# Strassen rounds of a decoder step: two products accumulated onto read-out PSUM banks, and the order of the seven products changed

## The chip, the cores and the metric

The kernel runs on one NeuronCore of one Trainium2 chip, alone. The metric is device time in microseconds (us) of one execution; several executions are timed and the median is given. Beside the times there is one profiled execution, whose trace is what the rows below are taken from.

## What is computed

One decoder layer for 544 tokens (512 of a prompt, 32 of eight sample streams of 4), all in fp32:

```
h = rmsnorm(x);  proj = h @ w_in
att = differential attention(q, k, v);  y = Mamba-2 mixer(conv(xbc), dt, z)
x = x + concat(att, y) @ w_out
hf = rmsnorm(x)
g = hf @ w_gate ; u = hf @ w_up            # 2048 x 5632 each
g = causal conv of width 3 along the tokens (g)
x = x + (silu(g) * u) @ w_down             # 5632 x 2048
y = rmsnorm(x)
```

The change touches only the three large products of the MLP, `w_gate`, `w_up` and `w_down`, which take the last 1,470 us or so of the span of 2441.0 us.

## The kernel before

**Precision.** A product of fp32 accuracy is made of three TensorE passes. Each operand is split in a high part `hi` (a rounded copy, made by ScalarE) and a low part `lo` (the remainder, a subtraction on VectorE); `mm` (line 157) is called for hi x hi, lo x hi and hi x lo. A weight block of 128x1024 goes through `split2` (lines 1067 to 1069): `whi` on ScalarE, then `wlo` on VectorE. Three `whi` and three `wlo` buffers exist, so the weights of three products can be ready or in use at a time.

**Rounds.** Each MLP product is computed in rounds of Strassen's method in Winograd's form. A round (`wino`, line 1113) takes a 2x2 arrangement of weight blocks and a 2x2 arrangement of activation blocks (two halves of 272 tokens each) and forms four output blocks with seven block products instead of eight. The activation blocks `B11, T1, T2, B21, T3, B22, T4` (`T` are sums of blocks) stay in SBUF for many rounds; the weight sums are formed anew for each round by the generator `wino_weights` (line 1071), from four quarters that a DMA brings: `a11`, `s1 = a21+a22`, `s2 = s1-a11`, `a12`, `a11-a21`, `a12-s2`, `a22`, in the order in which the products use them. The first two sums of a round are on VectorE (`wx<-wx`), on GpSimd (POOL) only for the first two rounds of each sequence; the later two (`wx<-wraw,wx`, `wx<-wx,wraw`) are on VectorE.

There are 68 rounds: 44 for gate and up (22 pairs; a product is 8 blocks deep, 24 matmuls of 128x272), then three passes over `w_down` with 8 rounds each (`PASSES`, 7, 7 and 6 blocks deep, 21, 21 and 18 matmuls a product). One product takes one PSUM bank. The bank comes from a ring of three (`half()`, tag `po`) for six of the products; `T1` has a bank of its own, `sB` and `sc` in turn.

**Combining the products.** Let P(X) be the product with block X. The four outputs are (0,0) = P(B11)+P(B21); (1,1) = ud+P(T1); (0,1) = ub+P(T1)+P(B22); (1,0) = ud+P(T4), with ub = P(B11)+P(T2) and ud = ub+P(T3). The order of the seven calls and of the adds between them is that of lines 1132 to 1140.

`take` adds the base and uses the output: `gate` (line 1261) adds on VectorE into one of the temporaries `ua`, `ub`, `ud` and hands that to the conv (lines 305 and 306 scale it into `pre`); `up` (line 1265) adds and multiplies into `sg`; in the down passes `take` (line 1369) adds the bank to the residual `x` on VectorE and then the base on POOL.

**Order.** TensorE runs in the order of the program. VectorE, ScalarE, POOL and the DMA queue are ordered by a scheduler that works with priorities, except in the first gate round, where the order of the code holds (`manual_schedule`, line 1304). In the first gate round the last 272-token blocks of the activations are still being split (`build`, line 1225; `first_gate`, line 1270, calls it between the products). At the end of the gate and up rounds and of each down pass the activation blocks are replaced: `put_blocks` (line 1289) is called after each product of the last round, loads the new block of that product through five `st` buffers and splits it (`xl<-st`, and the like) at a low priority. Such a round and the one behind it are called a changeover below. There are three.

Of the kernel before, what the change touches and what calls it, by code (L numbers as in the profile page):

```python
# [25 lines left out]
HT = TOK // 2  # L26
# [73 lines left out]
def body(tc, i, o):  # L100
# [55 lines left out]

    def mm(out, lhsT, rhs, start=True, stop=True):
        T.matmul(out, lhsT=lhsT, rhs=rhs, start=start, stop=stop)  # L158
        n, m = rhs.free_size(), lhsT.free_size()
        side.now += 4 * n / 2400 if rhs.dtype == F32 else max(n / 2400, m / 1200)  # L160
# [892 lines left out]

    BLK = ("B11", "T1", "T2", "B21", "T3", "B22", "T4")
    sB = tc.alloc_tile_pool(name="sB", bufs=1)
# [15 lines left out]
    def wino_weights(srcs, n):  # L1071
# [19 lines left out]
        for at, src in enumerate(srcs):  # L1091
            a11, a21, a22 = nxt
            e = G if at < 2 else V
            yield split(a11)
            s1 = tmp()
            add(e, s1, a21, a22)
            s2 = tmp()
            sub(e, s2, s1, a11)
            yield split(s1)
            a12 = load(src, 3, "wraw", 2, wp)  # L1100
            yield split(s2)
            sub(V, a21, a11, a21)
            yield split(a12)
            sub(V, s2, a12, s2)
            yield split(a21)
            if at + 1 < len(srcs):
                nxt = loads(srcs[at + 1])
            yield split(s2)
            yield split(a22)
# [3 lines left out]
    def wino(q, take, after=None):  # L1113


        c = half(("sB", "sc")[turn_[0] % 2])
        turn_[0] += 1
        ua, ub, ud = uc

        def prod(t, po):  # L1120
            w = wnext()
            for j in range(q):
                h, l = (x[:, j % 2] for x in blk[t][j // 2])
                k = slice(j * P, (j + 1) * P)
                mm(po[:, 0:HT], w[0][:, k], h, j == 0, False)
                mm(po[:, 0:HT], w[1][:, k], h, False, False)
                mm(po[:, 0:HT], w[0][:, k], l, False, j == q - 1)
                side.poll()
            if after is not None:
                after(t)  # L1130
            return po[:, 0:HT]
        A.activation(ua, prod("B11", half()), AF.Copy)
        c = prod("T1", c)
        V.tensor_tensor(ub, prod("T2", half()), ua, op=ALU.add)
        take(0, 0, ua, prod("B21", half()), ua)
        V.tensor_tensor(ud, prod("T3", half()), ub, op=ALU.add)  # L1136
        V.tensor_tensor(ub, c, ub, op=ALU.add)
        take(1, 1, ud, c, ua)
        take(0, 1, ub, prod("B22", half()), ub)
        take(1, 0, ud, prod("T4", half()), ud)  # L1140

# [43 lines left out]
    def x1_tile(m):  # L1185
# [9 lines left out]
        elif m == NK - 1:  # L1195
            ch = [wnext(), wnext()]
            po = [half(), half()]
            for k in range(NK):
                for hf in range(2):
                    mm3(po[hf], kslice(ch, k), ms[k], hf, k == 0, k == NK - 1)  # L1200
                if k % 4 == 3:
                    blk[BLK[3 + k // 4]] = [xslot(k - 3 + jj) for jj in range(4)]
                    if k < NK - 1:
                        build(BLK[3 + k // 4], range(3))
            wfill()
# [50 lines left out]
    def begin(g):  # L1256
        sG = u["gate"]
        u["sg"] = sg = u["pool"].tile([P, 2, 2, HT], F32, name="sg", tag="sg", bufs=2)
        u["cv"] = [conv(sG, "f", LF, 3, *(u[n][:, 2 * g + k] for n in ("par", "prev", "tail")), sg[:, k], 1) for k in range(2)]

    def gate(n, hf, base, po, c):
        V.tensor_tensor(c, po, base, op=ALU.add)
        u["cv"][n](hf, c)

    def up(n, hf, base, po, c):
        sg = u["sg"][:, n, hf]
        V.tensor_tensor(c, po, base, op=ALU.add)
        V.tensor_tensor(sg, c, sg, op=ALU.mult)

    def first_gate(t):  # L1270
        if t == "B11":
            squares(NK - 1, u["last"])
            wfill()
            build("B21", [3])
            build("T3", [3])
        elif t == "T1":
            build("B22", [3])
        elif t == "T2":
            build("T4", range(4))
            sO.release()  # L1280
            open_up()
        elif t == "B21":
            u["order"].close()
            begin(0)
# [75 lines left out]
    for p, q in enumerate(PASSES):  # L1360
# [4 lines left out]
        for m in range(NK // 2):  # L1365
# [3 lines left out]
            def take(n, hf, base, po, c):  # L1369
                x = x1_of(p, 2 * m + n)[:, hf]  # L1370
                V.tensor_tensor(x, po, x, op=ALU.add)
                add(G, x, base, x)
            after = None
# [192 lines left out]
```

## Time and profile before

| | us |
|---|---|
| runs timed: 2440.73, 2443.16, 2433.55; median | 2440.73 |
| the profiled execution's own time | 2442.75 |
| its span, first to last instruction | 2441.0 |
| TensorE matmuls busy (of the span) | 2355.5 (96%) |
| VectorE busy | 2083.3 (85%) |
| ScalarE busy | 1141.7 (47%) |
| POOL busy | 722.6 (30%) |

The busy shares are averages over the span. A row of a timeline is: start in us from the span's start, duration in us, engine, line of the kernel, operation, what is written `<-` what is read with partitions x elements, the count of merged instructions, and in brackets the idle time of the engine just before it and what ended that. PE is TensorE, DVE VectorE, ACT ScalarE. A mean clock of 1.00 is 2.4 GHz, one of 0.50 would be 1.2 GHz. A stretch with TensorE busy throughout has no wait in it, whatever the other engines show.

### The profile page before, as it was taken

What the parts mean: (1) busy time and instruction counts of PE and PEld (TensorE: products, weight loads), DVE (VectorE), ACT (ScalarE), POOL (GpSimd) and SP (SyncE); (2) the same over time, 40 slices, a digit from 0 to 9 for tenths busy, and PEclk for the clock granted to TensorE, in tenths of its full rate; (3) what the DMA queues carried; (4) which work ended last, traced back from release to release, by engine and by line L of the source; (5) the groups of instructions that cost most, each with busy time, mean ns of one, the idle gap of its engine ahead of it and who ended that gap; (6) DMA issues with size and microseconds to landing.
All of it is one profiled execution on the core that took longest, in us unless ns stands there. A gap on an engine that the chain in (4) does not pass through costs nothing.

```text
span 2441.0 us, 46377 instructions
## 1 busy us (share of the span) xinstructions
PE 2355.5 (96%) x18184; PEld 2302.7 (94%) x18184; DVE 2083.3 (85%) x2893; ACT 1141.7 (47%) x1651; POOL 722.6 (30%) x655
## 2 busy tenths in 40 slices
PE   8999999999999999899999999999999899899997
PEld 7989898998999999899999999999999899898997
DVE  8686778787877556999999999999999988989986
ACT  5645345656565323444444444444444534435345
POOL 4243233333321113522222222322221222423223
PEclk9999999999999999899999999999999999999999
DMA  5434444444555443243434343333433755747432
GB/s 163 130 126 129 157 155 145 149 155 147 165 161 160 151 146 115 87 142 110 140 112 141 123 141 116 130 131 116 139 111 131 220 173 178 228 152 229 141 113 83
DMA packets 172285, 350.45 MB, mean 144 GB/s; under 512 B 19474, under 2 KB 89874, under 8 KB 172066
## 3 DMA queue, kind: packets, MB, share of 16 engines
q1 hardware_dynamic: 171250, 346.65, 44.1%
q8 instruction: 143, 2.34, 0.4%
q10 hardware_dynamic: 816, 0.84, 0.1%
q14 instruction: 76, 0.62, 0.1%
HBM read 293.07 MB, written 54.35 MB: 142 GB/s over the span
## 4 chain that ended last, share of the span: by engine, by line
PE 59%; DVE 7%; DMA 2%; issue 2%; ACT 1%; POOL 0%; DVEq 0%; SPq 0%; ACTq 0%; POOLq 0%
PE po L158 58%; DVE wlo L1062 2%; DVE xl L1062 1%; DMA st<-hTs 1%; DVE wx L1062 1%; ACT whi L1068 0%; DMA wraw<-in_w_gu 0%; DMA xr<-in_xT 0%; DVE ssq L1423 0%; DMA st<-hB 0%; PE pos L158 0%; PE scs L158 0%; ACT xh L1068 0%; DVE acc L316 0%; DMA wraw<-in_w_down 0%
## 5 line engine op out<-in xcount | busy, mean ns | idle before, releaser
L158 PE MATMUL po<-xh,whi 128*128 128x272 f32 x3968 | 1160.3, 292 | 18.4 <-ACT whi L150 5.2
L158 PE MATMUL po<-xh,wlo 128*128 128x272 f32 x3968 | 1152.6, 290 | 13.5 <-DVE wlo L1062 11.9
L158 PE MATMUL po<-xl,whi 128*128 128x272 f32 x3968 | 1150.1, 290 | 5.5 <-DVE xl L254 5.5
L158 PEld LDWEIGHTS po<-xh,whi 128*128 128x128 f32 x3968 | 756.4, 191 | 27.2 <-ACT whi L1068 8.0
L158 PEld LDWEIGHTS po<-xh,wlo 128*128 128x128 f32 x3968 | 754.8, 190 | 22.6 <-DVE wlo L1062 14.8
L158 PEld LDWEIGHTS po<-xl,whi 128*128 128x128 f32 x3968 | 755.3, 190 | 6.4 <-DVE xl L254 6.4
L1068 ACT ACTIVATE whi<-wx 128x1024 fp32r<-128x1024 f32 (+2 forms) x340 | 343.2, 1010 | 474.8 <-PE po L158 448.5
L1062 DVE TENSOR_TENSOR wlo<-wx,whi 128x1024 fp32r<-128x1024 f32 (+2 forms) x340 | 437.5, 1287 | 51.6 <-ACT whi L1068 49.4
L1068 ACT ACTIVATE whi<-wraw 128x1024 fp32r<-128x1024 f32 (+2 forms) x136 | 136.9, 1006 | 191.5 <-PE po L158 182.2
L151 DVE TENSOR_TENSOR wlo<-wraw,whi 128x1024 fp32r<-128x1024 f32 (+1 forms) x132 | 166.3, 1265 | 61.4 <-ACT whi L150 61.0
L1062 DVE TENSOR_TENSOR wlo<-wraw,whi 128x1024 fp32r<-128x1024 f32 (+2 forms) x136 | 170.6, 1254 | 7.4 <-ACT whi L1068 5.3
L1062 DVE TENSOR_TENSOR wx<-wraw,wx 128x1024 f32<-128x1024 f32 (+2 forms) x136 | 172.2, 1269 | 5.4 <-POOL wx L1062 2.9
L150 ACT ACTIVATE whi<-wraw 128x1024 fp32r<-128x1024 f32 (+1 forms) x132 | 127.8, 976 | 95.4 <-PE po L158 73.0
L699 POOL TENSOR_TENSOR kvl<-kv,kvh 128x512 fp32r<-128x512 f32 x64 | 105.0, 1641 | 178.4 <-ACT kvh L697 171.5
L158 PE MATMUL po<-T2h,whi 128*128 128x272 f32 x512 | 148.9, 291 | 5.3 <-DVE xr L1191 4.7
L158 PE MATMUL po<-B11h,whi 128*128 128x272 f32 x512 | 148.1, 289 | 5.7 <-DVE u L1136 5.7
L158 PE MATMUL po<-T2h,wlo 128*128 128x272 f32 x512 | 149.5, 292 | 3.3 <-DVE wlo L1062 3.3
L158 PE MATMUL po<-T2l,whi 128*128 128x272 f32 x512 | 149.2, 291 | 0.0
L158 PE MATMUL po<-T1h,wlo 128*128 128x272 f32 x512 | 147.7, 289 | 1.5 <-DVE wlo L1062 1.5
L158 PE MATMUL po<-B11h,wlo 128*128 128x272 f32 x512 | 148.3, 290 | 0.0
L158 PE MATMUL po<-B11l,whi 128*128 128x272 f32 x512 | 148.3, 290 | 0.0
L158 PE MATMUL po<-T1l,whi 128*128 128x272 f32 x512 | 147.5, 288 | 0.0
(406 smaller groups left out, 4196.4 us busy)
## 6 DMA issues: line engine op xcount, KB each, us to landing
wx<-in_w_gu SPq DMA_DIRECT2D x88, 512.0 KB, 3.9
wraw<-in_w_gu SPq DMA_DIRECT2D x88, 512.0 KB, 3.9
wraw<-in_w_in SPq DMA_DIRECT2D x84, 512.0 KB, 3.8
kv<-in_kc SPq DMA_DIRECT2D x128, 128.0 KB, 2.2
kv<-in_vc SPq DMA_DIRECT2D x128, 128.0 KB, 2.7
wraw<-in_w_out SPq DMA_DIRECT2D x32, 512.0 KB, 3.9
wx<-in_w_down SPq DMA_DIRECT2D x32, 448.0 KB, 3.6
wraw<-in_w_down SPq DMA_DIRECT2D x32, 448.0 KB, 3.6
```

What stands on the lines that cost most here:

```text
L150: A.activation(hi[:, c], raw[:, c], AF.Copy)
L151: V.tensor_tensor(lo[:, c], raw[:, c], rd(hi[:, c]), op=ALU.subtract)
L158: T.matmul(out, lhsT=lhsT, rhs=rhs, start=start, stop=stop)
L699: e.tensor_tensor(l[:, s], src[:, s], rd(h)[:, s], op=ALU.subtract)
L1062: e.tensor_tensor(out, a, b, op=op)
L1068: A.activation(h, src, AF.Copy)
```

## The change

The order of the products becomes B11, T1, T2, T3, B21, B22, T4, and the weight sums are made in that order. P(B21) is accumulated onto the bank that holds P(B11), without clearing it, and P(B22) onto the bank that holds P(T1); ScalarE copies P(B11) to `ua` as before, and VectorE reads P(T1) for (1,1) before P(B22) is added there. So (0,0) is ready in PSUM, and (0,1) lacks only ub. The add `ub = c + ub` of every round is gone (68 of them), and `take(0, 0)` gets no base: in gate and up its VectorE add is gone (44), in the down passes its POOL add (24). The two banks that are accumulated onto come from two pairs in turn, (`sB`, `sc`) and (`pb`, `sA`); the ring of three now serves T2, T3 and T4. The matmuls keep their number and shapes.

```diff
--- before.py
+++ after.py
@@ -154,8 +154,8 @@
             return hi, lo
         return hi, lo, part
 
-    def mm(out, lhsT, rhs, start=True, stop=True):
-        T.matmul(out, lhsT=lhsT, rhs=rhs, start=start, stop=stop)
+    def mm(out, lhsT, rhs, start=True, stop=True, more=False):
+        T.matmul(out, lhsT=lhsT, rhs=rhs, start=start, stop=stop, skip_group_check=more)
         n, m = rhs.free_size(), lhsT.free_size()
         side.now += 4 * n / 2400 if rhs.dtype == F32 else max(n / 2400, m / 1200)
 
@@ -1051,7 +1051,7 @@
 
 
 
-    BLK = ("B11", "T1", "T2", "B21", "T3", "B22", "T4")
+    BLK = ("B11", "T1", "T2", "T3", "B21", "B22", "T4")
     sB = tc.alloc_tile_pool(name="sB", bufs=1)
     blk = {}
     for t in BLK[:3]:
@@ -1100,9 +1100,9 @@
             a12 = load(src, 3, "wraw", 2, wp)
             yield split(s2)
             sub(V, a21, a11, a21)
+            yield split(a21)
+            sub(V, s2, a12, s2)
             yield split(a12)
-            sub(V, s2, a12, s2)
-            yield split(a21)
             if at + 1 < len(srcs):
                 nxt = loads(srcs[at + 1])
             yield split(s2)
@@ -1113,31 +1113,33 @@
     def wino(q, take, after=None):
 
 
-        c = half(("sB", "sc")[turn_[0] % 2])
+
+        b, c = (half(t) for t in (("sB", "sc"), ("pb", "sA"))[turn_[0] % 2])
         turn_[0] += 1
         ua, ub, ud = uc
 
-        def prod(t, po):
+        def prod(t, po=None, more=False):
+
+            po = half() if po is None else po
             w = wnext()
             for j in range(q):
                 h, l = (x[:, j % 2] for x in blk[t][j // 2])
                 k = slice(j * P, (j + 1) * P)
-                mm(po[:, 0:HT], w[0][:, k], h, j == 0, False)
-                mm(po[:, 0:HT], w[1][:, k], h, False, False)
-                mm(po[:, 0:HT], w[0][:, k], l, False, j == q - 1)
+                mm(po[:, 0:HT], w[0][:, k], h, j == 0 and not more, False, more)
+                mm(po[:, 0:HT], w[1][:, k], h, False, False, more)
+                mm(po[:, 0:HT], w[0][:, k], l, False, j == q - 1, more)
                 side.poll()
             if after is not None:
                 after(t)
             return po[:, 0:HT]
-        A.activation(ua, prod("B11", half()), AF.Copy)
-        c = prod("T1", c)
-        V.tensor_tensor(ub, prod("T2", half()), ua, op=ALU.add)
-        take(0, 0, ua, prod("B21", half()), ua)
-        V.tensor_tensor(ud, prod("T3", half()), ub, op=ALU.add)
-        V.tensor_tensor(ub, c, ub, op=ALU.add)
-        take(1, 1, ud, c, ua)
-        take(0, 1, ub, prod("B22", half()), ub)
-        take(1, 0, ud, prod("T4", half()), ud)
+        A.activation(ua, prod("B11", b), AF.Copy)
+        t1 = prod("T1", c)
+        V.tensor_tensor(ub, prod("T2"), ua, op=ALU.add)
+        V.tensor_tensor(ud, prod("T3"), ub, op=ALU.add)
+        take(1, 1, ud, t1, ua)
+        take(0, 0, None, prod("B21", b, True), ua)
+        take(0, 1, ub, prod("B22", c, True), ub)
+        take(1, 0, ud, prod("T4"), ud)
 
     x1d = dr.tile([NK, P, 2, HT], F32, name="x1d")
     hB = dr.tile([NF // 2, P, 2, 2, HT], F32, name="hB")
@@ -1199,9 +1201,10 @@
                 for hf in range(2):
                     mm3(po[hf], kslice(ch, k), ms[k], hf, k == 0, k == NK - 1)
                 if k % 4 == 3:
-                    blk[BLK[3 + k // 4]] = [xslot(k - 3 + jj) for jj in range(4)]
+                    t = ("B21", "T3", "B22", "T4")[k // 4]
+                    blk[t] = [xslot(k - 3 + jj) for jj in range(4)]
                     if k < NK - 1:
-                        build(BLK[3 + k // 4], range(3))
+                        build(t, range(3))
             wfill()
             for hf in range(2):
                 evac(hf, po[hf])
@@ -1258,28 +1261,31 @@
         u["sg"] = sg = u["pool"].tile([P, 2, 2, HT], F32, name="sg", tag="sg", bufs=2)
         u["cv"] = [conv(sG, "f", LF, 3, *(u[n][:, 2 * g + k] for n in ("par", "prev", "tail")), sg[:, k], 1) for k in range(2)]
 
+    def summed(base, po, c):
+        if base is None:
+            return po
+        V.tensor_tensor(c, po, base, op=ALU.add)
+        return c
+
     def gate(n, hf, base, po, c):
-        V.tensor_tensor(c, po, base, op=ALU.add)
-        u["cv"][n](hf, c)
+        u["cv"][n](hf, summed(base, po, c))
 
     def up(n, hf, base, po, c):
         sg = u["sg"][:, n, hf]
-        V.tensor_tensor(c, po, base, op=ALU.add)
-        V.tensor_tensor(sg, c, sg, op=ALU.mult)
+        V.tensor_tensor(sg, summed(base, po, c), sg, op=ALU.mult)
 
     def first_gate(t):
         if t == "B11":
             squares(NK - 1, u["last"])
             wfill()
+            build("T3", [3])
             build("B21", [3])
-            build("T3", [3])
         elif t == "T1":
             build("B22", [3])
         elif t == "T2":
             build("T4", range(4))
             sO.release()
             open_up()
-        elif t == "B21":
             u["order"].close()
             begin(0)
 
@@ -1369,7 +1375,8 @@
             def take(n, hf, base, po, c):
                 x = x1_of(p, 2 * m + n)[:, hf]
                 V.tensor_tensor(x, po, x, op=ALU.add)
-                add(G, x, base, x)
+                if base is not None:
+                    add(G, x, base, x)
             after = None
             if m == NK // 2 - 1:
                 after = last_weights if p == len(PASSES) - 1 else lambda t: put_blocks(t, p + 1)
```

Line numbers from here to the prediction are those of the kernel before, unless the row is of the changed kernel; there the four lines of the round are 1135 (copy of P(B11)), 1137 (T2), 1138 (T3), `summed` is 1267, the product of `up` 1275 and the add of the down passes 1377.

First place: VectorE in the first gate round, from the weight sum `a11-a21` (`wx_11160`) on. `xl3` belongs to block B21, `xl7` to T3, `xl11` to B22. Before:

```order
L1062 TENSOR_TENSOR wx_11160<-wraw_11158,wx_11160 128x1024
L1062 TENSOR_TENSOR wlo_11376<-wraw_11330,whi_11375 128x1024
L1062 TENSOR_TENSOR xl3_11209<-kp3_9491,xh3_11208 128x544
L1062 TENSOR_TENSOR xl7_11253<-kp3_9491,xh7_11252 128x544
L1062 TENSOR_TENSOR xl11_11291<-kp3_9491,xh11_11290 128x544
L1062 TENSOR_TENSOR wx_11170<-wraw_11330,wx_11170 128x1024
L1062 TENSOR_TENSOR wlo_11415<-wx_11160,whi_11414 128x1024
L1134 TENSOR_TENSOR u1_9478<-po_11412,u0_9477 128x272
L1262 TENSOR_TENSOR u0_9477<-po_11462,u0_9477 128x272
L1062 TENSOR_TENSOR wlo_11470<-wx_11170,whi_11469 128x1024
L1062 TENSOR_TENSOR wlo_11522<-wx_11162,whi_11521 128x1024
L1253 TENSOR_TENSOR ssq2_9483<-ssq2_9483,rstd_9585 128x272 x2
```

Of the change:

```order
L1062 TENSOR_TENSOR wx_11160<-wraw_11158,wx_11160 128x1024
L1062 TENSOR_TENSOR wlo_11376<-wx_11160,whi_11375 128x1024
L1062 TENSOR_TENSOR xl7_11253<-kp3_9491,xh7_11252 128x544
L1062 TENSOR_TENSOR xl3_11209<-kp3_9491,xh3_11208 128x544
L1062 TENSOR_TENSOR xl11_11291<-kp3_9491,xh11_11290 128x544
L1062 TENSOR_TENSOR wx_11170<-wraw_11330,wx_11170 128x1024
L1062 TENSOR_TENSOR wlo_11415<-wraw_11330,whi_11414 128x1024
L1137 TENSOR_TENSOR u1_9478<-po_11412,u0_9477 128x272
L1062 TENSOR_TENSOR wlo_11480<-wx_11170,whi_11479 128x1024
L1138 TENSOR_TENSOR u2_9479<-po_11472,u1_9478 128x272
L1062 TENSOR_TENSOR wlo_11522<-wx_11162,whi_11521 128x1024
L1267 TENSOR_TENSOR u0_9477<-po_11345,u2_9479 128x272
```

The weights `a11-a21` are now split directly behind the subtraction that makes them, and those of `a12` later; before it was the other way round. The read of P(T1) for (1,1) (L1267 on `po_11345`) now stands ahead of the norm's two products and reciprocals, behind two weight splits.

Second place: VectorE in the last changeover, the first round of the last down pass, from the low part of the weights of B22 on. `xl12` to `xl14` are the new block T4. Before:

```order
L1062 TENSOR_TENSOR wlo_25977<-wx_25833,whi_25976 128x768
L1062 TENSOR_TENSOR xl10_11289<-st_25824,xh10_11288 128x544
L1134 TENSOR_TENSOR u1_9478<-po_25944,u0_9477 128x272
L1062 TENSOR_TENSOR wlo_26002<-wx_25789,whi_26001 128x768
L1062 TENSOR_TENSOR xl12_11323<-st_25860,xh12_11322 128x544
L1062 TENSOR_TENSOR xl13_11325<-st_25864,xh13_11324 128x544
L1062 TENSOR_TENSOR xl14_11327<-st_25868,xh14_11326 128x544
L1371 TENSOR_TENSOR rstd_9585<-po_25969,rstd_9585 128x272
L1062 TENSOR_TENSOR wlo_26029<-wraw_25970,whi_26028 128x768
L1136 TENSOR_TENSOR u2_9479<-po_26000,u1_9478 128x272
```

Of the change:

```order
L1062 TENSOR_TENSOR wlo_25737<-wx_25593,whi_25736 128x768
L1137 TENSOR_TENSOR u1_9478<-po_25704,u0_9477 128x272
L1062 TENSOR_TENSOR xl12_11323<-st_25620,xh12_11322 128x544
L1062 TENSOR_TENSOR wlo_25762<-wx_25549,whi_25761 128x768
L1062 TENSOR_TENSOR xl13_11325<-st_25624,xh13_11324 128x544
L1062 TENSOR_TENSOR xl14_11327<-st_25628,xh14_11326 128x544
L1138 TENSOR_TENSOR u2_9479<-po_25729,u1_9478 128x272
L1377 TENSOR_TENSOR x1_1_21774<-po_25655,x1_1_21774 128x272
L1062 TENSOR_TENSOR wlo_25785<-wraw_25730,whi_25784 128x768
L1377 TENSOR_TENSOR rstd_9585<-po_25654,rstd_9585 128x272
```

Before, the bank for B22 is freed by L1134 (T2 read), which stands ahead of the three splits of block T4. In the change B22 is accumulated onto `po_25655`, which is read by L1377, behind these splits and L1138.

Third place: VectorE in a steady up round (the last but one pair), from the read of P(T2) on. Before:

```order
L1134 TENSOR_TENSOR u1_9478<-po_21027,u0_9477 128x272
L1062 TENSOR_TENSOR wx_21061<-wraw_21059,wx_21061 128x1024
L1062 TENSOR_TENSOR wlo_21066<-wx_20924,whi_21065 128x1024
L1267 TENSOR_TENSOR u0_9477<-po_21058,u0_9477 128x272
L1062 TENSOR_TENSOR wx_21162<-wx_21160,wraw_21059 128x1024
L1062 TENSOR_TENSOR wlo_21097<-wx_20816,whi_21096 128x1024
L1268 TENSOR_TENSOR sg_20709<-u0_9477,sg_20709 128x272
L1136 TENSOR_TENSOR u2_9479<-po_21095,u1_9478 128x272
L1137 TENSOR_TENSOR u1_9478<-po_20965,u1_9478 128x272
L1267 TENSOR_TENSOR u0_9477<-po_20965,u2_9479 128x272
```

Of the change:

```order
L1137 TENSOR_TENSOR u1_9478<-po_20871,u0_9477 128x272
L1062 TENSOR_TENSOR wlo_20910<-wx_20768,whi_20909 128x1024
L1062 TENSOR_TENSOR wx_21002<-wx_21000,wraw_20903 128x1024
L1138 TENSOR_TENSOR u2_9479<-po_20902,u1_9478 128x272
L1267 TENSOR_TENSOR u0_9477<-po_20810,u2_9479 128x272
L1062 TENSOR_TENSOR wlo_20941<-wx_20664,whi_20940 128x1024
L1275 TENSOR_TENSOR sg_20557<-u0_9477,sg_20557 128x272
L1275 TENSOR_TENSOR sg_20557<-po_20809,sg_20557 128x272
```

Before, two weight sums and two splits stand between the reads of T2 and T3; in the change one split and one sum, and the read of P(T1) (L1267 on `po_20810`) follows T3's at once.

## Rows read from the trace of the kernel before

**Rows 1.** Windows of the MLP's stages: length, busy us (instructions) per engine, clock, DMA.

```profile
960.00:1075.00 115.00, 100.43 (x742) 98.53 (x741) 107.91 (x123) 49.27 (x68) 52.06 (x40) 0.94 0.28 94
1075.00:1900.00 825.00, 825.00 (x6588) 825.00 (x6587) 804.62 (x1022) 358.31 (x431) 224.66 (x231) 1.00 0.38 128
1900.00:1950.00 50.00, 39.81 (x282) 38.33 (x281) 45.46 (x62) 29.21 (x46) 13.01 (x7) 0.93 0.75 237
...
2070.00:2112.00 42.00, 33.85 (x242) 31.96 (x241) 40.36 (x52) 23.76 (x36) 18.77 (x11) 0.96 0.77 237
2112.00:2234.00 122.00, 122.00 (x980) 122.00 (x979) 107.03 (x125) 52.51 (x65) 36.90 (x29) 1.00 0.58 185
2234.00:2264.00 30.00, 22.75 (x159) 21.47 (x158) 28.22 (x37) 14.48 (x22) 10.75 (x10) 0.94 0.82 251
```

**Rows 2.** Waits of PE on reads of PSUM banks: total us, times, longest.

```profile
PE po L158 <- DVE u L1136: 5.7, 3, 3.4
...
PE po L158 <- DVE rstd L1371: 2.9, 2, 1.9
...
PE po L158 <- DVE u L1134: 2.7, 1, 2.7
```

**Rows 3.** Timeline of DVE in a steady up round.

```profile
1317.68 0.43 DVE L1134 TENSOR_TENSOR u<-po,u 128x272 f32<-128x272 f32 x1
1318.03 1.21 DVE L1062 TENSOR_TENSOR wx<-wraw,wx 128x1024 f32<-128x1024 f32 x1
1319.16 1.21 DVE L1062 TENSOR_TENSOR wlo<-wx,whi 128x1024 fp32r<-128x1024 f32 x1
...
1323.27 0.43 DVE L1136 TENSOR_TENSOR u<-po,u 128x272 f32<-128x272 f32 x1
1323.73 0.44 DVE L1137 TENSOR_TENSOR u<-po,u 128x272 f32<-128x272 f32 x1
```

**Rows 4.** Timeline of PE, the last matmul of product T3 of the same round.

```profile
1321.02 0.29 PE L158 MATMUL po<-xl,whi 128*128 128x272 f32 x1
```

**Rows 5.** Timeline of DVE in the first gate round and at the start of the next.

```profile
981.29 1.22 DVE L1062 TENSOR_TENSOR wx<-wraw,wx 128x1024 f32<-128x1024 f32 x1
...
993.24 3.79 DVE L1062 TENSOR_TENSOR wlo<-wx,whi 128x1024 fp32r<-128x1024 f32 x2
...
1004.87 1.21 DVE L1062 TENSOR_TENSOR wlo<-wraw,whi 128x1024 fp32r<-128x1024 f32 x1
1006.01 0.43 DVE L1136 TENSOR_TENSOR u<-po,u 128x272 f32<-128x272 f32 x1
```

**Rows 6.** Timeline of ACT, the high part of the fourth product's weights in the first round.

```profile
981.45 1.04 ACT L1068 ACTIVATE whi<-wraw 128x1024 fp32r<-128x1024 f32 x1
```

**Rows 7.** Timeline of DVE in the first changeover.

```profile
1907.94 1.09 DVE L1062 TENSOR_TENSOR wx<-wraw,wx 128x896 f32<-128x896 f32 x1 [2.86 <-POOL wx L1062]
```

**Rows 8.** Timeline of DVE in the last changeover.

```profile
2254.81 2.23 DVE L1062 TENSOR_TENSOR wlo<-wx,whi 128x768 fp32r<-128x768 f32 x1
...
2258.87 0.43 DVE L1371 TENSOR_TENSOR rstd<-po,rstd 128x272 f32<-128x272 f32 x1
```

**Rows 9.** Timeline of PE in the last changeover: B22 starts, T4 starts, next round starts.

```profile
2255.03 0.36 PE L158 MATMUL po<-xh,whi 128*128 128x272 f32 x1 [2.73 <-DVE u L1134]
...
2259.44 0.36 PE L158 MATMUL po<-xh,whi 128*128 128x272 f32 x1 [1.94 <-DVE rstd L1371]
...
2260.24 0.43 PE L158 MATMUL po<-xl,whi 128*128 128x272 f32 x1
2260.47 0.43 PE L158 MATMUL po<-xh,whi 128*128 128x272 f32 x1
...
2263.19 0.39 PE L158 MATMUL po<-B11h,whi 128*128 128x272 f32 x1
```

**Rows 10.** Timeline of DVE in the second changeover.

```profile
2104.18 0.43 DVE L1371 TENSOR_TENSOR rstd<-po,rstd 128x272 f32<-128x272 f32 x1
```

**Rows 11.** Timeline of PE in the second changeover: the next round starts.

```profile
2108.61 0.36 PE L158 MATMUL po<-B11h,whi 128*128 128x272 f32 x1 [0.98 <-DVE u L1136]
```

## Prediction

> **What bounds the kernel now.** I read the windows of the stages first, then PE's waits, then the timelines around the few places where PE waits. The windows say nearly everything: from 1075 to 1900 us PE is busy for 825.00 of 825 us at full clock, and between two changeovers for 122.00 of 122 [rows 1]. There TensorE sets the pace, 122 us over 980 matmuls, 124.5 ns each, so that a product of 24 takes 2.99 us, one of 21 takes 2.61 and one of 18 takes 2.24. VectorE is close behind (804.62 of 825 us), yet nothing waits for it. The change keeps every matmul, so in these stretches it can give nothing, however many adds go. What it can give lies in four stretches, the first rounds (960 to 1075) and the three changeovers: PE idles there for 14.57, 10.19, 8.15 and 7.25 us, 40.2 in all, at mean clocks of 0.93 to 0.96 [rows 1]. VectorE is busy for 91 to 96% of these four. Of the waits there, 11.3 us are put down to VectorE's reads of PSUM banks [rows 2], which the change rearranges; the others are mostly for weights and blocks not yet split.
>
> **The adds.** Gone are 44 x 2 + 24 = 112 adds on VectorE and 24 on POOL. From the start of one such add to the next instruction it is 0.35 us (1317.68 to 1318.03) [rows 3], so VectorE is relieved by 112 x 0.35 = 39 us. About 100 of the 112 lie in stretches where PE never waits and are worth nothing there: PE itself is the cover. Were PE faster by 3% there, VectorE's 97.5% would be the bound and these adds would count.
>
> **The steady rounds: 0.** One wait is new: P(B22) goes onto P(T1)'s bank and cannot start before VectorE has read it. In an up round before, T3's last matmul ends at 1321.02 + 0.29 = 1321.31 [rows 4] and P(T1) is first read at 1323.73 to 1324.17 [rows 3], 2.86 us later. In the changed order only B21 lies between T3 and B22, so B22 would start at 1321.02 + 0.12 + 2.99 = 1324.13, 2.82 us behind T3's end. With VectorE's old order this would be a wait of about 0.1 us in each up round. But in the new order only one split and one sum stand between the reads of T2 and T3: 0.35 + 1.13 + 1.13 = 2.6 us by starts [rows 3], under a product, so T3 is read as soon as it is there and T1 0.8 us behind its end. Margin 2 us; I take 0.
>
> **The first rounds: -1.** The change has two costs here. The fourth product's weights are now a11-a21, whose sum VectorE makes at 981.29 [rows 5]; ScalarE's split of a12 started at 981.45, beside it, and took 1.04 [rows 6]. It must now come behind the sum, and VectorE's `wlo` behind that: +1.0. Then B22 waits for the read of P(T1) behind two splits, which took 3.79 us beside POOL [rows 5], and T3's read; I put this at up to +1.5. Against them, VectorE, which works here without a pause until it has caught up, is relieved by 8 adds in four rounds, -2.8. The second round's B11 waited 3.4 us for the read of T3 [rows 2], and with a bank of its own it no longer does; but its `wlo` ran from 1004.87 and was only 0.35 us ahead of that read (1006.01 to 1006.44) [rows 5], so the wait changes its name and gives about 0.5. Sum -1; ends +2.5 (costs alone) and -6.7 (adds, the wait wholly).
>
> **First changeover: -1.** VectorE idled for 2.86 us until POOL had made a sum [rows 7]; in the changed order POOL's sum stands ahead of a product of `sg` instead of behind it, which can give up to 2.9, and two adds go, 0.7. Against that B22 of the first down round now waits, as in the next paragraph. Ends -3.6 and +3.
>
> **Last changeover: +1.5.** Before, B22 started at 2255.03, released by the read of T2, and T4 at 2259.44, released by a read that ended behind T4's three block splits; the next round started at 2263.19 [rows 9]. Now B22 itself waits for P(T1), whose read stands behind those splits and T3's read: the old read began at 2258.87 [rows 8]; add 0.35 for T3's, 0.43 for T1's own, take off 0.35 for an add that goes in the round before: 2259.3. Then two products still have to run, where before one was left. At full clock they take 4.5 us and end at 2263.8; after the old wait the pace fell to 227 ns a matmul (2260.24 to 2260.47) [rows 9], 1.2 GHz, and with the first of the two at that pace they take 4.1 + 2.2 and end at 2265.6. So +0.6 to +2.4. VectorE may also come earlier, as its split of 2.23 us [rows 8] was stretched by POOL: -1. I take +1.5, nearer the slow clock, since PE's idle time before B22 grows from 2.7 to 7 us.
>
> The Trainium skill (PSUM — Partial Sum Buffer, section "PSUM bank collisions raise a hardware error") says that waits on PSUM are to be set by bank, because two engines may not be in one bank at once. By it the two changeover terms stand as they are; without such a wait B22 could start earlier and the sum would be about 3 us lower. The rows of before show waits on ring banks only, so that this one is real is no row's proof.
>
> **Second changeover: +1.5.** The same order with 21 matmuls a product. The last of the reads began at 2104.18 [rows 10]; with the same steps T1's read ends at 2104.6, B22 and T4 end at 2109.8 at full clock and at 2112.0 with one at half, where the next round started at 2108.61, itself held for 0.98 us by a read [rows 11] that now falls away. So +1.2 to +3.4, or -1 if VectorE comes earlier.
>
> **Sum.** -1 - 1 + 1.5 + 1.5 = +1, against the profiled execution's 2442.75 us. That stands 2.0 above the median of the three runs, 2440.73, so the forecast is 2441 with the runs' own spread of 10 us, from 2433.55 to 2443.16, around it. The ends sum to about -12 and +11. A difference of 0.5%, 12 us, is about what can be told from no change for this kernel.
>
> **Rivals.**
> *The bank waits go and nothing stands behind them (faster).* The 11.3 us of bank waits [rows 2] go whole, and so does the 2.86 us idle, and VectorE's relief adds 2.8 in the first rounds: -17, 2424 us. For it: VectorE was named as the last releaser. Against it: where I looked, a split ended within 0.4 us of the read, and the same VectorE queue is late with it. A half of it, -8, is likelier than the whole.
> *B22's wait becomes the bound (slower).* Place: first down rounds of each pass. It decides where P(T1) is read later than one product behind T3. If some 7 us of idle time leave B22 and T4 both at 227 ns, a changeover costs 2 x 21 x (227 - 124.5) ns = 4.3 us beyond full clock and 1 us of the wait itself; three of them, nothing gained from POOL's sum, and the +2.5 of the first rounds make +18, 2459 us.
> *A small wait in every up round (slower).* If the scheduler's order made VectorE read T1 as late as before plus one split (2.86 + 1.13 against 2.8), 21 up rounds would lose 1.2 us each, +25, 2466 us. The new order in the third place speaks against it.
> *The change does nothing that the clock can tell.* That is the forecast: PE is the cover for nearly all of it.
>
> **How the numbers follow.** Forecast, within half a per cent, 0.77: it needs only that the steady stretches stay free of waits, which the rows show with 2 us to spare, and that the four short stretches do not change by half of what is idle in them. Faster rival to beyond 0.5%: 0.14. The two slower ones: 0.06 and 0.03. The range 2429 to 2451 takes in the ends of the terms and part of the spread of the runs, and half of the faster rival; outside are its far end and the slower rivals.
>
> **What the profile after would show.** PE at 825 of 825 us again in the gate and up rounds, with VectorE at about 95% where it was 97.5; no PE wait on the reads of T2 or T3 (1137, 1138); instead waits of B22's first matmul on 1377 in the three first down rounds and on 1267 in the first gate round; 112 fewer adds of 0.43 us. The sum of idle time in the four stretches should be 35 to 46 us. I am wrong if PE waits inside the steady rounds, if the pace of the accumulating matmuls differs from 124.5 ns, or if the idle time of the four stretches falls by 12 us or more.

## The result, and the profile after

The changed kernel takes 2476.15 us (median of 4 runs, 2474.85 to 2480.23) against 2439.64 us before, measured beside it: a ratio of 1.0152, 95% interval 1.0134 to 1.0171. It is slower by 36.5 us, where 2441 us, within half a per cent, was forecast. The profiled execution's span is 2474.5 us, 33.5 more than before.

The adds are gone as read from the code: VectorE runs 2781 instructions for 2893 and POOL 631 for 655. The time went elsewhere. First the windows of the changed kernel (length, busy us and instructions of PE, PEld, DVE, ACT, POOL, mean clock, DMA share, GB/s), which answer to [rows 1]; the last row holds most of the second changeover, which comes later here:

```profile
960.00:1075.00 115.00, 100.48 (x751) 98.51 (x750) 107.54 (x120) 50.73 (x68) 56.99 (x44) 0.96 0.30 100
1075.00:1900.00 825.00, 803.02 (x6377) 799.38 (x6376) 757.69 (x912) 347.89 (x418) 220.38 (x225) 1.00 0.36 124
...
2100.00:2150.00 50.00, 41.66 (x296) 40.47 (x297) 46.52 (x59) 25.35 (x39) 14.68 (x9) 0.93 0.78 244
```

The second line is the finding: 803.02 us busy where [rows 1] has 825.00. TensorE now stops inside the steady rounds, which no part of the sum had allowed for. The waits of PE say how often (us in total, times, longest); the last line is the same view of 1075 to 1900 us alone, where it is the only line:

```profile
PE po L158 <- ACT whi L1068: 28.2, 23, 3.5
PE po L158 <- DVE x L1377: 19.8, 3, 10.6
...
PE po L158 <- DVE u L1267: 6.3, 3, 2.9
...
PE po L158 <- ACT whi L1068: 22.0, 19, 1.2
```

There are 19 stops of 1.16 us in that window, one in each up round and none in a gate round. The timeline of PE in one up round shows where, and in the first changeover the longest stop of all. The first row is T3's last matmul, the second B21's last, the third B22's first; the fourth is B22's first in round 44:

```profile
1278.90 0.29 PE L158 MATMUL po<-xl,whi 128*128 128x272 f32 x1
...
1281.90 0.29 PE L158 MATMUL po<-xl,whi 128*128 128x272 f32 x1
1283.35 0.36 PE L158 MATMUL po<-xh,whi 128*128 128x272 f32 x1 [1.16 <-ACT whi L1068]
...
1970.83 0.56 PE L158 MATMUL po<-xh,whi 128*128 128x272 f32 x1 [10.64 <-DVE x L1377]
```

And VectorE in the same up round, which answers to [rows 3] (1137 reads T2, 1138 T3, and the 1267 behind it is the first read of P(T1)):

```profile
1269.49 1.59 DVE L305 TENSOR_TENSOR pre<-u,rstd 128x256 f32<-128x256 f32 x1
...
1274.98 1.22 DVE L1062 TENSOR_TENSOR wx<-wx 128x1024 f32<-128x1024 f32 x1
1276.12 1.22 DVE L1062 TENSOR_TENSOR wlo<-wraw,whi 128x1024 fp32r<-128x1024 f32 x1
1277.26 2.38 DVE L1062 TENSOR_TENSOR wx<-wraw,wx 128x1024 f32<-128x1024 f32 x1
1279.56 0.43 DVE L1137 TENSOR_TENSOR u<-po,u 128x272 f32<-128x272 f32 x1
1279.91 1.21 DVE L1062 TENSOR_TENSOR wlo<-wx,whi 128x1024 fp32r<-128x1024 f32 x1
1281.15 1.23 DVE L1062 TENSOR_TENSOR wx<-wx,wraw 128x1024 f32<-128x1024 f32 x1
1282.29 0.43 DVE L1138 TENSOR_TENSOR u<-po,u 128x272 f32<-128x272 f32 x1
1282.76 0.44 DVE L1267 TENSOR_TENSOR u<-po,u 128x272 f32<-128x272 f32 x1
```

T3 ended at 1278.90 + 0.29 = 1279.19. P(T1) was read until 1282.76 + 0.44 = 1283.20, 4.0 us later, and B22 began at 1283.35. It could have begun at 1281.90 + 0.12 = 1282.03: 1.32 us are lost. B22's own weights were ready by then: their low part was made from 1279.91 to 1281.12. The cause stands ahead of the reads: T2 ended at 1276.18 and was read only at 1279.56, 3.4 us late, behind a sum of 2.38 us.

The profile names ScalarE's `whi` as the releaser, since that split ended last before B22:

```profile
1276.21 1.06 ACT L1068 ACTIVATE whi<-wx 128x1024 fp32r<-128x1024 f32 x1 [0.36 <-PE po L158]
1279.27 1.06 ACT L1068 ACTIVATE whi<-wx 128x1024 fp32r<-128x1024 f32 x1 [2.00 <-PE po L158]
1282.23 1.06 ACT L1068 ACTIVATE whi<-wraw 128x1024 fp32r<-128x1024 f32 x1 [1.90 <-PE po L158]
```

It is not the cause. The weights of a round have two quarters straight from `wraw`, `a11` and `a12`; the one at 1282.23 is the next round's B11, and B22's own `whi` is the first of these rows. In the first experiment below the same split stands at the same place of the round and B22 starts ahead of it.

To see where all of it went I took, in the stretch of the 68 rounds, every gap between the starts of successive matmuls beyond the full pace of 124.5 ns, and summed them by round. That counts stops and slow clock alike; a round without a stop shows 0.24 us. "Up rounds" are the 19 odd rounds 5 to 41, less that 0.24 each; a changeover is taken here with one more round behind it, since some stops reach into that:

| | time, us | ratio to before, 95% | rounds 0-3 | 19 up rounds | three changeovers | all 68 rounds |
|---|---|---|---|---|---|---|
| before | 2439.64 | | 23.8 | 0 | 15.5 + 12.5 + 10.9 | 75.4 |
| the change | 2476.15 | 1.0152 [1.0134, 1.0171] | 22.7 | 26.5 | 20.6 + 14.1 + 14.2 | 110.0 |
| e1 B22 in a bank of its own | 2435.34 | 0.9970 [0.9957, 0.9984] | 19.5 | 0 | 14.2 + 10.2 + 10.7 | 67.0 |
| e2 ScalarE copies P(T1) out | 2438.45 | 0.9982 [0.9971, 0.9992] | 21.9 | 0 | 15.2 + 13.9 + 7.8 | 70.6 |
| e3 no product of `sg` on POOL | 2445.34 | 1.0011 [0.9997, 1.0024] | 20.2 | 0.2 | 18.8 + 13.4 + 14.1 | 78.6 |
| e4 B21 alone, old order | 2432.39 | 0.9961 [0.9945, 0.9976] | 20.0 | 0.2 | 13.3 + 10.7 + 8.2 | 64.4 |
| e5 B22 behind T4 | 2438.10 | 0.9985 [0.9975, 0.9995] | 19.6 | 0 | 17.0 + 12.5 + 10.7 | 71.6 |
| e6 both, old order, B22 behind T4 | 2447.46 | 1.0022 [1.0009, 1.0035] | 26.2 | 0.2 | 19.7 + 13.9 + 13.4 | 85.4 |
| e7 both, old order | 2582.05 | 1.0578 [1.0560, 1.0596] | 36.5 | 82.7 | 22.5 + 17.8 + 16.8 | 214.9 |
| e8 the order alone | 2440.79 | 1.0000 [0.9988, 1.0012] | 23.4 | 0.2 | 14.6 + 12.8 + 10.2 | 74.3 |

Each ratio is to runs of before on the same chip: 2441.78 us beside e1 to e4, 2441.00 beside e5 to e8. The columns on the right are of one profiled execution each, and that of e6 took 2452.94 us, 5.5 more than its median. Of the change's 34.6 us, 26.5 lie in the up rounds (1.40 each) and 10.0 in the changeovers; the first rounds gave back 1.1 and the last round 0.8.

### The profile page after: what moved, and what is told of

Its sections match the earlier page's. It is cut to its first block, busy times and chain, and to the rows that moved or that the text cites. A ratio compares the mean times of both kernels' runs of the same rounds, so it can differ in the third digit from the quotient of the medians.

```text
span 2474.5 us, 46027 instructions
## 1 busy us (share of the span) xinstructions
PE 2357.2 (95%) x18184; PEld 2301.9 (93%) x18184; DVE 2037.9 (82%) x2781; ACT 1141.5 (46%) x1651; POOL 692.5 (28%) x631
## 4 chain that ended last, share of the span: by engine, by line
PE 50%; DVE 4%; ACT 2%; DMA 2%; issue 1%; SPq 0%; DVEq 0%; ACTq 0%
PE po L158 50%; ACT whi L1068 1%; DMA st<-hTs 1%; DVE wlo L1062 1%; DMA st<-hB 1%; DVE xl L1062 0%; DVE ssq L1430 0%; DVE y L1412 0%; ACT u L1428 0%; DVE T2l L1062 0%; DVE B11l L1062 0%; DMA wraw<-in_w_last 0%; ACT xh L1068 0%; DVE x L1423 0%; DVE acc L316 0%
## 5 line engine op out<-in xcount | busy, mean ns | idle before, releaser
L158 PE MATMUL po<-xh,wlo 128*128 128x272 f32 x3968 | 1153.1, 291 | 10.9 <-DVE wlo L1062 9.0
L1062 DVE TENSOR_TENSOR wlo<-wx,whi 128x1024 fp32r<-128x1024 f32 (+2 forms) x340 | 427.2, 1257 | 63.2 <-ACT whi L1068 58.0
L1062 DVE TENSOR_TENSOR wx<-wraw,wx 128x1024 f32<-128x1024 f32 (+2 forms) x136 | 193.7, 1425 | 4.1 <-POOL wx L1062 2.0
L1062 DVE TENSOR_TENSOR wlo<-wraw,whi 128x1024 fp32r<-128x1024 f32 (+2 forms) x136 | 160.9, 1183 | 21.9 <-ACT whi L1068 21.7
```

What stands on the lines that cost most here:

```text
L158: T.matmul(out, lhsT=lhsT, rhs=rhs, start=start, stop=stop, skip_group_check=more)
L1062: e.tensor_tensor(out, a, b, op=op)
```

## The experiments

The theory was that B22 stops because VectorE still reads the bank it is to be added to, and that VectorE is late because weight sums stand ahead of T2's read. The rivals: adding a product onto a read-out bank is slow in itself; or the new order of products (with its new order of weight sums) is what costs.

**e1: B22 in a bank of its own.** The order and B21's accumulation stay.

```diff
+        V.tensor_tensor(ub, t1, ub, op=ALU.add)
         take(1, 1, ud, t1, ua)
         take(0, 0, None, prod("B21", b, True), ua)
-        take(0, 1, ub, prod("B22", c, True), ub)
+        take(0, 1, ub, prod("B22"), ub)
```

> The changed kernel, with the product of B22 back in a ring bank of its own and the add ub = P(T1) + ub back on VectorE; the new order and the accumulation of B21 stay. Bank wait (B22 waits for VectorE's late read of P(T1)): the 1.40 us of idle PE in each up round go (19 x 1.40 = 26.6 us), and most of the growth of the changeovers (about 10 us); 2434 to 2444 us. Order (the new order makes VectorE late, whatever bank is used): 2465 us or more. Accumulation (matmuls onto a bank that was read are slower, or hold TensorE up): about half of the loss stays, 2458 us, and the pace inside B21 is over 124.5 ns.

All of the loss is gone, and the kernel is a little faster than before. Its window of the steady rounds:

```profile
1075.00:1900.00 825.00, 825.00 (x6588) 825.00 (x6587) 793.70 (x980) 360.49 (x434) 240.03 (x229) 1.00 0.39 127
```

VectorE reads P(T1) at the same place as in the changed kernel (15.77 us after the start of an up round in both, with one more add behind it) and nobody waits. In round 44 the 10.64 us stop is gone too, but the round still loses 11.3 us beyond the full pace, where the changed kernel loses 14.1: other waits for what VectorE splits come instead, the longest in T3, for its weights:

```profile
1925.44 0.60 PE L158 MATMUL po<-xh,wlo 128*128 128x272 f32 x1 [3.47 <-DVE wlo L1062]
```

**e2: ScalarE copies P(T1) out**, so that the bank is free without VectorE; both accumulations and the order stay.

```diff
-        t1 = prod("T1", c)
+        A.activation(ud, prod("T1", c), AF.Copy)
         V.tensor_tensor(ub, prod("T2"), ua, op=ALU.add)
-        V.tensor_tensor(ud, prod("T3"), ub, op=ALU.add)
-        take(1, 1, ud, t1, ua)
+        V.tensor_tensor(ua, prod("T3"), ub, op=ALU.add)
+        take(1, 1, ua, ud, ud)
...
```

> The changed kernel, with P(T1) copied to SBUF by ScalarE as soon as it is there, and (1,1) made from that copy, so that the bank is free long before B22; both accumulations and the new order stay, VectorE has as many instructions. Bank wait: B22 finds the bank free, 2432 to 2444 us, with no idle PE in the steady rounds. Order: 2465 us or more. Accumulation: 2470 us or more, as both accumulations stay.

B22 is still added onto P(T1)'s bank, 68 times, and the steady rounds run without a stop. Accumulating is not slow in itself; waiting for VectorE's read is.

**e3: POOL's product of `sg` and `rstd` left out.** It is 44 instructions.

```diff
-        for n in range(2):
-            add(G, sg[:, n], sg[:, n], rstd_now[0], ALU.mult)
```

> The changed kernel without POOL's product of sg with the norm's factor (44 instructions; the up rounds then work with unscaled sg). In the up rounds POOL's 2.35 us stand beside VectorE's weight sum of 2.38 us, which takes 1.21 us alone, ahead of the reads of T2, T3 and T1. Bank wait with VectorE held by POOL: the read of T1 comes 1.17 us earlier, the idle time before B22 falls from 1.40 to 0.2 to 0.3 us; 19 to 20 rounds x 1.15 = 22 us less, 2450 to 2458 us. If the lateness is VectorE's own order alone: 2470 us or more.

The 19 stops went and the time fell by 31 us, more than expected: 26.3 came from the up rounds, where I had thought part of the lateness would remain, and the rest from rounds 0 to 3 and the changeovers (2.5 and 2.6). What POOL did to VectorE stands in these rows. First POOL in the changed kernel:

```profile
1269.03 1.76 POOL L1062 TENSOR_TENSOR sg<-sg,rstd 128x544 f32<-128x544 f32 x1 [0.58 <-ACT sg L319]
...
1276.21 2.35 POOL L1062 TENSOR_TENSOR sg<-sg,rstd 128x544 f32<-128x544 f32 x1
```

Then VectorE in the same round of e3 (its round starts 6.10 us earlier, at 1260.90):

```profile
1263.40 0.42 DVE L305 TENSOR_TENSOR pre<-u,rstd 128x256 f32<-128x256 f32 x1
...
1270.00 1.21 DVE L1062 TENSOR_TENSOR wx<-wraw,wx 128x1024 f32<-128x1024 f32 x1
1271.13 0.43 DVE L1137 TENSOR_TENSOR u<-po,u 128x272 f32<-128x272 f32 x1
```

The `wx` sum takes 1.21 us here and 2.38 beside POOL's second product. The scaling on 305 takes 0.42 here and, beside the first product (1269.49 in the changed kernel), 1.59. Two stretches of 1.17 us make T2's read 2.34 us later, 12.57 instead of 10.23 us after the round's start, and T1's read ends at 16.21 instead of 13.88. B22 can start at 15.03. So with POOL's two products it is late, without them it has 1.1 us to spare. The changeovers keep their stops (10.7 us is still the longest), so this product does not make those.

**e4: B21 alone**, in the order of before; B22 in a ring bank.

```diff
-        A.activation(ua, prod("B11", half()), AF.Copy)
+        A.activation(ua, prod("B11", b), AF.Copy)
...
-        take(0, 0, ua, prod("B21", half()), ua)
+        take(0, 0, None, prod("B21", b, True), ua)
```

> The kernel before with only the accumulation of B21 onto P(B11)'s bank, in the old order; (0,0) without its add; B22 in a ring bank. Bank wait: nothing new to wait for, since ScalarE alone reads P(B11) and does it at once; no idle PE in the steady rounds, 2432 to 2441 us. Accumulation: slower than before by 15 us or more. Order: 2432 to 2441 us too (the order is the old one).

It is the fastest kernel of the study, 9.4 us below the before measured beside it (2441.78). P(B11) is read by ScalarE while T1 runs, nearly two products before B21 wants the bank, so no wait comes of it in the steady rounds (in the first round B21 waited 0.31 us for that read). The gain lies in the changeovers (38.9 to 32.2 us) and the first rounds (23.8 to 20.0). Two things could make it there: VectorE and POOL have fewer adds, and B11 and B21 no longer take banks of the ring. No run tells the two apart.

A second set asked how the price goes with the distance between the read and B22.

**e5: B22 behind T4**, the changed kernel otherwise; all 112 adds stay gone.

```diff
-    BLK = ("B11", "T1", "T2", "T3", "B21", "B22", "T4")
+    BLK = ("B11", "T1", "T2", "T3", "B21", "T4", "B22")
...
-            yield split(s2)
             yield split(a22)
+            yield split(s2)
...
-        take(0, 1, ub, prod("B22", c, True), ub)
         take(1, 0, ud, prod("T4"), ud)
+        take(0, 1, ub, prod("B22", c, True), ub)
```

> The changed kernel with B22 and T4 exchanged (B11, T1, T2, T3, B21, T4, B22): both products are still accumulated and all 112 adds stay gone, but T1's bank is now wanted one product (3.0 us) later. Bank wait: in an up round T1's read ended 16.21 us after the round's start, and B22 would now start at 18.04, so nothing is waited for in the 19 steady up rounds (-26.5 us), and the waits of 10.81 and 7.07 us for this bank in two changeovers shrink by up to 3 us each: 2438 to 2448 us. Accumulating costs by itself, wherever it stands: as the changed kernel, about 2476 us.

One product more between them takes the whole loss away. The reads of P(T1) by the down rounds still stop PE, in two changeovers:

```profile
PE po L158 <- DVE x L1377: 8.0, 2, 4.3
```

**e6: both accumulated in the order B11, T1, T2, B21, T3, T4, B22.** It is e4 with B22 added onto P(T1)'s bank and exchanged with T4.

```diff
...
-        V.tensor_tensor(ub, c, ub, op=ALU.add)
         take(1, 1, ud, c, ua)
-        take(0, 1, ub, prod("B22", half()), ub)
         take(1, 0, ud, prod("T4", half()), ud)
+        take(0, 1, ub, prod("B22", cb, True), ub)
```

> Both products accumulated in the order B11, T1, T2, B21, T3, T4, B22 (the order of before but for T4 and B22), all 112 adds gone. Bank wait: with B21 alone accumulated T3 was read from 16.82 us after an up round's start and T1 until 17.72; B22 would start at 18.04, so the steady rounds run without a stop with 0.2 us to spare, and the changeovers are those of B21 alone or a little shorter: 2426 to 2436 us. If the spare is not enough, 0.2 to 0.5 us a round would be lost in 19 rounds: up to 2442 us. Accumulating costs by itself: 2460 us or more.

The steady rounds do run without a stop on the 0.3 us there is (P(T1) is read until 17.71 us after the round's start, B22 starts at 18.04). The changeovers were forecast wrong, and 2447 us lies above both the 2426 to 2436 and the 2442 expected: in the profiled execution they lose 14.8 us against e4 and the first rounds 6.2, nearly all at B22, where VectorE comes later than in a steady round:

```profile
PE po L158 <- DVE u L1264: 15.5, 2, 7.9
PE po L158 <- DVE x L1375: 13.4, 3, 5.6
```

A margin read in a steady round does not hold where the same engine splits new blocks.

**e7: both accumulated in the order of before**, B22 directly behind T3.

```diff
...
-        V.tensor_tensor(ub, c, ub, op=ALU.add)
         take(1, 1, ud, c, ua)
-        take(0, 1, ub, prod("B22", half()), ub)
+        take(0, 1, ub, prod("B22", cb, True), ub)
         take(1, 0, ud, prod("T4", half()), ud)
```

> Both products accumulated in the order of before, B22 directly behind T3, so that T1's bank is wanted as soon as T3 is done. Bank wait: B22 would start 15.03 us after the round's start, but T1 is read until about 17.7 us in up rounds and until about 16.1 us in gate rounds, so about 2.8 us are lost in each of 19 up rounds and 1.2 us in each of 20 gate rounds, some 75 us, and more in the changeovers: 2500 to 2530 us. If the chip lets the accumulation start before the bank has been read, or the price is the accumulation's and not the wait's: 2440 to 2476 us.

The time, 2582.05 us, lies beyond the 2500 to 2530 expected. The stops are as long as expected (B22 at 17.86 for 15.03 us after the start of an up round, at 16.30 in a gate round), but the up rounds lose 4.35 us each, not 2.8, and the first rounds and changeovers 31 us more than before. The waits of PE between 1075 and 1900 us:

```profile
PE po L158 <- DVE u L1263: 45.3, 17, 2.7
PE po L158 <- ACT whi L1068: 18.7, 17, 1.1
```

Here the profile names the read itself in the up rounds. The read of P(T1) and then the timeline of PE at such a stop show the other 1.5 us:

```profile
1310.68 0.44 DVE L1263 TENSOR_TENSOR u<-po,u 128x272 f32<-128x272 f32 x1
...
1308.31 0.29 PE L158 MATMUL po<-xl,whi 128*128 128x272 f32 x1
1311.27 0.56 PE L158 MATMUL po<-xh,whi 128*128 128x272 f32 x1 [2.67 <-DVE u L1263]
...
1313.90 0.43 PE L158 MATMUL po<-xl,whi 128*128 128x272 f32 x1
1314.12 0.43 PE L158 MATMUL po<-xh,whi 128*128 128x272 f32 x1
...
1314.67 0.28 PE L158 MATMUL po<-xh,whi 128*128 128x272 f32 x1
1314.79 0.29 PE L158 MATMUL po<-xh,wlo 128*128 128x272 f32 x1
```

Behind the stop the matmuls start 0.22 to 0.23 us apart, and only from 1314.5 on 0.12 to 0.13 again: the granted clock is at its lower level, 1.2 GHz, for some 3 us.

**e8: the order alone**, nothing accumulated, every add of before.

```diff
-        take(1, 1, ud, t1, ua)
-        take(0, 0, None, prod("B21", b, True), ua)
-        take(0, 1, ub, prod("B22", c, True), ub)
+        V.tensor_tensor(ub, t1, ub, op=ALU.add)
+        take(0, 0, ua, prod("B21"), ua)
+        take(1, 1, ud, t1, ua)
+        take(0, 1, ub, prod("B22"), ub)
```

> The new order alone, nothing accumulated, all adds of before. Bank wait: no product shares a bank with a late read, so steady rounds stay without a stop; own bank for B22 gave 2435 us with B21 accumulated, and B21 alone in the old order 2432 us, so the order alone should cost about 3 us: 2438 to 2448 us. If the order is what costs the time: 2465 us or more.

The order by itself costs and gains nothing, so the rival that blamed it is out. Each kernel taken against the before beside it, the steps from before to the change are: the order -0.2 us (e8), then B21's accumulation -6.2 (e1 against e8), then B22's +43 (the change against e1). They sum to the change's +36.5 by the way they are taken. The one independent look at a part, B21 alone in the old order (e4), gives -9.4. Wherever B22 was put on P(T1)'s bank, in e2, e5 and e6 too, the kernel was not faster than e1 and e4, which leave that bank alone.

## Why the prediction was wrong

**What bounds the kernel, and the adds.** Right: where PE is busy throughout, VectorE's relief gives nothing. In e4 and e1 the gain lies only in the first rounds and the changeovers, as said.

**The steady rounds: 0.** This step failed. It said: "only one split and one sum stand between the reads of T2 and T3: 0.35 + 1.13 + 1.13 = 2.6 us by starts, under a product, so T3 is read as soon as it is there and T1 0.8 us behind its end. Margin 2 us; I take 0." The distance was right: 1282.29 - 1279.56 = 2.73 us. But it was counted from a read of T2 that was taken to be on time, and that read itself was 3.4 us late. A queue that is behind by 3.4 us and then needs nearly a product from one read to the next stays behind: T3 was read 3.1 us after its end and T1 was done 4.0 us after it, where 2.8 were allowed. The step looked at what stands between the two reads, and not at what stands ahead of the first. The trace of before could have warned: there T1's read came 2.86 us behind T3's end, as the same step says, so VectorE was behind in the up rounds already. In the round of [rows 3] T2 ended at 1315.00 + 0.29 = 1315.29 and was read at 1317.68, 2.39 us late, behind a sum that took 2.42 us beside POOL:

```profile
1315.00 0.29 PE L158 MATMUL po<-T2l,whi 128*128 128x272 f32 x1
1315.34 2.42 DVE L1062 TENSOR_TENSOR wx<-wx 128x1024 f32<-128x1024 f32 x1
```

The new order then moved one more sum (`wx<-wraw,wx`, behind T2's read before) ahead of that read, which is the last 1 us of the 3.4.

The third rival, "a small wait in every up round", with "1.2 us each, +25, 2466 us" and a chance of 0.03, is what happened: 19 rounds of 1.40 us, 26.5. Its lateness of 2.86 + 1.13 us was met too (4.0), but not its reason: what was added stands ahead of T2's read, not between T3's end and T1's. The argument against it, that "the new order in the third place speaks against it", was the failed step again.

**The first rounds: -1.** Measured -1.1 (23.8 to 22.7), and that is luck. B22 waited 0.59, 2.80 and 1.17 us in rounds 0, 1 and 3, some 4.6 in all where up to 1.5 was allowed; the wait behind the first round, which was to give 0.5, went from 3.41 to 0.78 us.

**The changeovers: -1, +1.5 and +1.5.** They came to +5.1, +1.6 and +3.3. The first is the term that was mis-sized. There I had set a gain from POOL's sum against B22's wait; but B22 waited 2.94 us in round 43 and 10.64 in round 44, where VectorE ran five groups of block splits (`xl<-st`) between 1955 and 1970 us, the last two of them around T2's read (1137) and ahead of the reads of T3 and T1:

```profile
1961.89 2.96 DVE L1062 TENSOR_TENSOR xl<-st,xh 128x544 fp32r<-128x544 f32 x2
1964.77 0.43 DVE L1137 TENSOR_TENSOR u<-po,u 128x272 f32<-128x272 f32 x1
...
1967.65 2.33 DVE L1062 TENSOR_TENSOR xl<-st,xh 128x544 fp32r<-128x544 f32 x4
...
1970.26 0.42 DVE L1377 TENSOR_TENSOR x<-po,x 128x272 f32<-128x272 f32 x1
```

The second rival had named this wait. Yet it is not worth its length: with B22 in a bank of its own (e1) both waits go, 13.6 us, but the first changeover falls only from 20.6 to 14.2 us. The second number, +1.6, is near its forecast by luck: B22 waited 2.21 us, about what T4 and the next round had waited before (0.92 and 0.98), and the growth is a wait of T3 for its weights (1.39 to 3.48 us). In the last changeover B22's wait grew from 2.73 to 6.91 us, as forecast ("from 2.7 to 7"); waits for split weights add the rest. e1 takes 13.8 us out of the three together, so B22's bank costs more there than the balance of +10 shows; B21's accumulation gives some back. The 11.3 us of bank reads in the prediction leave out a line of the same view, 1.5 us on `u` of L1267 in the first changeover; only the first rival's sum would grow by it.

**That a matmul onto a bank waits for the read of it.** The prediction had no row for this. Now there are two: in the changed kernel P(T1)'s read ends at 1283.20 and B22 starts at 1283.35; in e7 B22 starts 0.15 us behind the read as well. The Trainium skill (PSUM — Partial Sum Buffer, section "PSUM bank collisions raise a hardware error") asks for such waits by bank and quadrant, or more simply by bank; the trace agrees that one is there, 0.15 us from read to matmul. Reader and writer use the same columns here, so no run tells bank from address.

**Signs named beforehand.** Of the marks that would show the prediction wrong, "PE waits inside the steady rounds" came true. The pace of the accumulating matmuls stayed at 124.5 ns. The waits of B22 on 1377 in the three first down rounds (10.64, 2.21 and 6.91 us) and on 1267 in the first gate round (0.59) came as named. The idle time of the four stretches, taken between the same points of the rounds, is 48.6 us, outside the 35 to 46 named.

## What to carry to other kernels

An accumulation onto a bank that another engine reads first moves that read from "some time before the ring comes round" to a due time. Before costing it at nothing, follow the reader's queue back to the last point where it was idle and add up everything from there, in the steady state and in the stages where that engine has extra work; the distance between two of its reads says nothing about how late the first one is. Take first the bank whose reader is early (P(B11), read by ScalarE: -9 us), and put work that needs no such bank in between for the other (B22 behind T4: -38 us against the change), or leave that one alone: here it gained nothing at any place that was tried.

## What the runs showed of the hardware

A sum with two SBUF inputs on VectorE and a product with two SBUF inputs on POOL do not run beside each other. `wlo` on VectorE ran from 1276.12 to 1277.34; POOL's product, issued at 1276.21, took until 1278.56, and VectorE's next sum, from 1277.26, until 1279.64. Each ended 1.2 or 1.1 us behind the end of the one before it, so they ran in turn. The Trainium skill (SBUF — State Buffer, section "Who interferes with whom") says that a VectorE instruction with two SBUF inputs contends with a GpSimd instruction that reads SBUF, for ports that one of them holds exclusively; these rows agree. At 1.17 us for each of POOL's two products it was just enough to turn a margin of 1.1 us into a stop of 1.3.

Some stops cost more than their length and others did not, and the length does not tell them apart. Behind the 1.16 us in the changed kernel the granted clock stayed at 1.00 (1283.30 to 1289.40); behind the 2.67 us in an up round of e7 it was 0.66 on average over 4.8 us, with the first matmuls at the 1.2 GHz level, and each such round lost 1.5 us more. But behind a stop of 2.77 us in the second round of e7, also after a stretch without a stop (15.20 of 15.20 us busy), it stayed at 1.00. The first two rows are that stop and the stretch behind it, the other three from around the stop of 2.67 us:

```profile
1023.40:1026.20 2.80, 0.03 (x2) 0.05 (x1) 2.66 (x5) 1.06 (x1) 0.00 (x0) 1.00 0.01 1
1026.20:1031.00 4.80, 4.80 (x38) 4.80 (x39) 2.84 (x5) 1.06 (x1) 0.47 (x1) 1.00 0.66 214
...
1293.40:1308.60 15.20, 15.20 (x122) 14.97 (x120) 15.02 (x17) 7.62 (x11) 5.50 (x7) 1.00 0.23 70
1308.60:1311.20 2.60, 0.00 (x0) 0.00 (x0) 2.49 (x4) 1.06 (x1) 0.00 (x0) 0.97 0.00 0
1311.20:1316.00 4.80, 4.73 (x26) 4.76 (x27) 1.58 (x3) 0.00 (x1) 0.00 (x0) 0.66 0.65 205
```

What stays open: e4 and e1 gain 6.7 and 3.8 us in the changeovers and about 4 in the first rounds, but which of the waits there would fall next was not tried, nor what decides whether the clock falls behind a stop.
